# Gate and up projections of a streaming encoder: sixteen of twenty-two column tiles by seven block products on a pre-normed x, and a down projection over all its outputs at once

## The chip, the cores and the metric

The kernel runs on one core of one Trainium2 chip, in one launch. The metric is the time on the device in microseconds (us); the kernel before takes 2091.73 us, the median of three runs (2091.29 to 2091.8). TensorE (PE in the profile) multiplies matrices into PSUM, eight banks of 128 rows by 512 fp32; VectorE (DVE), ScalarE (ACT) and GpSimd (POOL) work element by element; SyncE (SP) issues most of the DMAs. Each engine works through its own queue in order and waits for the others at semaphores.

## What is computed

Two layers on x of 512 frames by 1024 features. Each has a half-step SwiGLU feed-forward block (FFN), a mixer (three attention variants between two projections) and a second FFN; a last RMSNorm follows. The FFN, to which the change belongs:

```python
def rmsnorm(x, g):
    y = x * rsqrt(mean(x * x, axis=-1, keepdims=True) + EPS)
    return y * g

def swiglu(x, w_gate, w_up, w_down):          # 1024 x 2816, 1024 x 2816, 2816 x 1024
    return (silu(x @ w_gate) * (x @ w_up)) @ w_down

x = x + 0.5 * swiglu(rmsnorm(x, ffn1_norm), ffn1_w_gate, ffn1_w_up, ffn1_w_down)
...
x = x + 0.5 * swiglu(rmsnorm(x, ffn2_norm), ffn2_w_gate, ffn2_w_up, ffn2_w_down)
```

Everything is float32. The kernel reaches that precision with three passes of the rounded type fp32r: a value v is split into vh (v rounded) and vl = v - vh, and a product is the sum of wh*xh, wh*xl and wl*xh.

## The kernel before

x stands transposed: eight tiles x[k] of 128 features by 512 frames (KD = 8), beside them the split halves xh[k] and xl[k]. The hidden width of 2816 is 22 column tiles of 128 (KF = 22).

**Weights.** `plan` lists every weight unit in the order of use. `load_unit` (lines 109 to 131) takes the next: one DMA on SP's queue brings 128 x 1024 fp32 (512 KB) into `raw`, ACT copies it to `wh` (line 125), DVE subtracts to get `wl` (line 130). All of these tiles share eight buffers (`WBUFS`), and `wunit` keeps two units ahead of the one in use.

**One product.** `mm3` (lines 144 to 148) is three matmuls, each with a weight load of 128 x 128 (PEld in the profile) and, in the FFN, a moving operand of 128 x 512.

**One FFN** (lines 257 to 329). The gain is applied to x before the split, but 1/rms, which differs from frame to frame, is not: it is kept in `rbc` and multiplied in at the end. Gate and up are made in column groups (`UP_GROUPS`: two tiles, then four at a time). While the first group runs, POOL ends the sum of squares, `norm_stats` sums it over the partitions by matmuls (`ps_st`, line 210), and `norm_rows` broadcasts it (`ps_bc`, line 220). `evict` (lines 270 to 278) takes a tile's gate and up from PSUM: two multiplies by `rbc`, a silu on ACT, a product, and the split of the hidden tile into `fh` and `fl`. The down product follows in two halves of four output tiles (`DOWN_GROUPS`), each over all 22 hidden tiles; `norm_tile` then adds to the sum of squares and splits the new x for the next stage. The last FFN of the net makes its output with frames on the partitions (`last_down`) and puts the eight transposes of x for that (`token_x`) among the first group's matmuls.

**Order.** The program is written stage by stage; the framework's scheduler decides in which order the instructions of neighbouring steps stand on each engine, and pools with a fixed number of buffers decide what waits for what.

Of the kernel before, what the change touches and what calls it, by code (L numbers as in the profile page):

```python
# [9 lines left out]
F32 = mybir.dt.float32  # L10
# [19 lines left out]
UP_GROUPS = [(0, 2)] + [(j, 4) for j in range(2, KF, 4)]  # L30
DOWN_GROUPS = [(0, 4), (4, 4)]
# [18 lines left out]
class Net:  # L50
# [19 lines left out]
    def plan(self):  # L70
# [9 lines left out]
        def ffn(which, l, last=False):  # L80
# [3 lines left out]
            if last:  # L84
                yield from cols("down", a[f"{which}_w_down"][l], KF, 0, D)
                return
            for m, nm in DOWN_GROUPS:
                yield from cols("down", a[f"{which}_w_down"][l], KF, m * P, nm * P)

        for l in range(self.depth):  # L90
# [16 lines left out]
            yield from ffn("ffn2", l, l == self.depth - 1)  # L107

    def load_unit(self):
# [4 lines left out]
        name, src, nk, n = u  # L114
        m = nk * n
# [15 lines left out]
        self.ahead.append((name, v(wh), v(wl)))  # L131

# [18 lines left out]
    def constants(self):  # L151
# [21 lines left out]
        self.gains = keep.tile([P, P], F32, name="gains")  # L173
# [56 lines left out]
    def start(self, xp):  # L230
        nc = self.nc
        self.xt = [xp.tile([P, NT, 256], F32, name=f"xt{q}") for q in range(4)]
# [24 lines left out]
    def ffn(self, next_norm, begin=False):  # L257
        nc = self.nc
        with self.tc.tile_pool(name="ff", bufs=1, reuse_waits="tile") as fp:
            fh = [fp.tile([P, T], F32R, name=f"fh{j}") for j in range(KF)]  # L260
            fl = [fp.tile([P, T], F32R, name=f"fl{j}") for j in range(KF)]
            if not next_norm:
                self.rows = [fp.tile([P, D], F32, name=f"row{t}") for t in range(NT)]

            if begin:
                self.start(fp)
                self.first_x(0, ("ffn1_norm", 0))
                self.first_x(1, ("ffn1_norm", 0))

            def evict(j, gate, up):  # L270
                g = fp.tile([P, T], F32, name="g", tag="g", bufs=2)
                u = fp.tile([P, T], F32, name="u", tag="u", bufs=2)
                nc.vector.tensor_mul(g, gate, self.rbc)
                nc.scalar.activation(g, g, AF.Silu)
                nc.vector.tensor_mul(u, up, self.rbc)
                nc.vector.tensor_mul(u, u, g)  # L276
                nc.scalar.activation(fh[j], u, AF.Copy)  # L277
                nc.vector.tensor_sub(fl[j], u, f32(fh[j]))

            first = True  # L280
            for j, nj in UP_GROUPS:
                ps = {}
# [732 lines left out]
```

## Time and profile before

| | kernel before |
|---|---|
| three runs | 2091.29, 2091.73, 2091.8 us |
| the profiled execution | 2092.02 us; its span is 2090.2 us, so 1.8 us lie around it |
| TensorE busy | 2055.3 us (98%), 9801 matmuls, each with its load |
| VectorE busy | 1109.7 us (53%) |
| ScalarE busy | 830.7 us (40%) |
| GpSimd busy | 231.2 us (11%) |
| chain that ended last | PE 84%, DVE 8%, ACT 3% |

The four FFNs take about seven tenths of the span; the two mixers lie at about 390 to 700 and 1420 to 1735 us. A matmul's duration in the profile (0.40 us at 512 columns) is longer than the distance to the next one's start, since matmuls are pipelined; costs on TensorE are therefore read from starts.

### The profile page before, as it was taken

What the parts mean: (1) busy time and instruction counts of PE and PEld (TensorE: products, weight loads), DVE (VectorE), ACT (ScalarE), POOL (GpSimd) and SP (SyncE); (2) the same over time, 40 slices, a digit from 0 to 9 for tenths busy, and PEclk for the clock granted to TensorE, in tenths of its full rate; (3) what the DMA queues carried; (4) which work ended last, traced back from release to release, by engine and by line L of the source; (5) the groups of instructions that cost most, each with busy time, mean ns of one, the idle gap of its engine ahead of it and who ended that gap; (6) DMA issues with size and microseconds to landing.
All of it is one profiled execution on the core that took longest, in us unless ns stands there. A gap on an engine that the chain in (4) does not pass through costs nothing.

```text
span 2090.2 us, 25620 instructions
## 1 busy us (share of the span) xinstructions
PE 2055.3 (98%) x9801; PEld 1709.2 (82%) x9801; DVE 1109.7 (53%) x2000; ACT 830.7 (40%) x1398; POOL 231.2 (11%) x279
## 2 busy tenths in 40 slices
PE   7999999999999999999999999999999999999998
PEld 6888888898887888888888888889988888888886
DVE  4444433599986444543254454236999863544423
ACT  4222222376675322322232233225666843322222
POOL 2000000113433100000010000001233330000000
PEclk9999999999999999999999999999999999999999
DMA  4333323322212333333333333223222123333322
GB/s 137 91 94 98 91 94 98 89 74 61 68 54 65 91 98 94 91 99 93 91 91 100 91 91 100 92 90 85 79 59 56 51 83 99 95 97 91 100 92 91
DMA packets 112230, 183.09 MB, mean 88 GB/s; under 512 B 6242, under 2 KB 45484, under 8 KB 112108
## 3 DMA queue, kind: packets, MB, share of 16 engines
q1 hardware_dynamic: 111132, 179.59, 29.2%
q8 instruction: 77, 1.26, 0.3%
q10 hardware_dynamic: 864, 1.57, 0.2%
q14 instruction: 45, 0.37, 0.1%
q0 software_dynamic: 112, 0.30, 0.0%
HBM read 179.34 MB, written 2.10 MB: 87 GB/s over the span
## 4 chain that ended last, share of the span: by engine, by line
PE 84%; DVE 8%; ACT 3%; issue 2%; DMA 1%; POOL 1%; DVEq 0%; POOLq 0%; ACTq 0%; SPq 0%
PE ps_f L147 15%; PE ps_f L148 15%; PE ps_f L146 15%; PE ps_d L146 8%; PE ps_d L148 7%; PE ps_d L147 7%; PE ps_p L146 2%; PE ps_p L147 2%; PE ps_p L148 2%; PE ps_s L776 1%; PE ps_w L147 1%; PE ps_w L148 1%; PE ps_w L146 1%; PE ps_pt L449 1%; DVE isc L551 1%
## 5 line engine op out<-in xcount | busy, mean ns | idle before, releaser
L130 DVE TENSOR_TENSOR wl<-raw,wh 128x1024 fp32r<-128x1024 f32 (+5 forms) x323 | 388.1, 1202 | 840.6 <-PE ps_f L147 450.8
L125 ACT ACTIVATE wh<-raw 128x1024 fp32r<-128x1024 f32 (+5 forms) x346 | 355.5, 1028 | 836.0 <-DMA raw<-in_ffn_w_down 321.7
L146 PE MATMUL ps_f<-xh,wh 128*128 128x512 f32 x1408 | 558.6, 397 | 1.3 <-ACT xh L203 1.3
L147 PE MATMUL ps_f<-xl,wh 128*128 128x512 f32 x1408 | 558.1, 396 | 0.6 <-DVE xl L204 0.5
L148 PE MATMUL ps_f<-xh,wl 128*128 128x512 f32 x1408 | 557.3, 396 | 0.0
L147 PEld LDWEIGHTS ps_f<-xl,wh 128*128 128x128 f32 x1408 | 265.1, 188 | 65.3 <-DVE xl L204 2.1
L146 PEld LDWEIGHTS ps_f<-xh,wh 128*128 128x128 f32 x1408 | 264.8, 188 | 64.7 <-ACT xh L203 1.6
L148 PEld LDWEIGHTS ps_f<-xh,wl 128*128 128x128 f32 x1408 | 265.1, 188 | 63.7
L148 PE MATMUL ps_d<-fh,wl 128*128 128x512 f32 x528 | 208.8, 396 | 0.0
L147 PE MATMUL ps_d<-fl,wh 128*128 128x512 f32 x528 | 208.8, 395 | 0.0
L146 PE MATMUL ps_d<-fh,wh 128*128 128x512 f32 x528 | 208.8, 395 | 0.0
L198 POOL TENSOR_TENSOR rbc<-rbc,sq 128x512 f32<-128x512 f32 x42 | 63.6, 1515 | 1095.5 <-ACT sq L197 1094.7
L146 PE MATMUL ps_p<-wh,xh 128*128 128x320 f32 (+3 forms) x448 | 145.3, 324 | 2.1 <-ACT itm L466 1.5
L147 PE MATMUL ps_p<-wl,xh 128*128 128x320 f32 (+3 forms) x448 | 140.6, 314 | 0.0
L148 PE MATMUL ps_p<-wh,xl 128*128 128x320 f32 (+3 forms) x448 | 140.5, 314 | 0.0
L147 PEld LDWEIGHTS ps_d<-fl,wh 128*128 128x128 f32 x528 | 99.3, 188 | 24.0
L148 PEld LDWEIGHTS ps_d<-fh,wl 128*128 128x128 f32 x528 | 99.3, 188 | 24.0
L146 PEld LDWEIGHTS ps_d<-fh,wh 128*128 128x128 f32 x528 | 99.3, 188 | 23.8
L277 ACT ACTIVATE fh<-u 128x512 fp32r<-128x512 f32 x88 | 55.1, 630 | 130.7 <-DVE u L276 130.3
L786 POOL TENSOR_SCALAR s<-s,sm 128x128 f32<-128x128 f32 (+3 forms) x128 | 77.3, 606 | 225.2 <-DVE sm L785 188.1
L784 ACT ACTIVATE s<-s,sm 128x128 f32<-128x128 f32 (+3 forms) x128 | 71.6, 560 | 45.9 <-DVE sm L782 44.7
L146 PEld LDWEIGHTS ps_p<-wh,xh 128*128 128x128 f32 x448 | 84.3, 188 | 4.6 <-ACT itm L466 3.0
(204 smaller groups left out, 2739.1 us busy)
## 6 DMA issues: line engine op xcount, KB each, us to landing
raw<-in_ffn_w_gate SPq DMA_DIRECT2D x88, 512.0 KB, 3.7
raw<-in_ffn_w_up SPq DMA_DIRECT2D x88, 512.0 KB, 3.7
raw<-in_ffn_w_down SPq DMA_DIRECT2D x88, 512.0 KB, 3.7
raw<-in_w_out SPq DMA_DIRECT2D x32, 256.0 KB, 2.9
raw<-in_w_in SPq DMA_DIRECT2D x16, 384.0 KB, 3.3
raw<-in_w_in SPq DMA_DIRECT2D x12, 512.0 KB, 4.0
raw<-in_w_in SPq DMA_DIRECT2D x12, 480.0 KB, 3.6
xt<-in_x SPq DMA_DIRECT2D x4, 512.0 KB, 9.4
```

The source lines that it names most:

```text
L125: nc.scalar.activation(wh[:, :m], raw[:, :m], AF.Copy)
L130: nc.vector.tensor_sub(wl[:, :m], raw[:, :m], f32(wh[:, :m]))
L146: mm(ps, sh, mh, start=first, stop=False)
L147: mm(ps, sh, ml, start=False, stop=False)
L148: mm(ps, sl, mh, start=False, stop=last)
L198: (engine or nc.gpsimd).tensor_add(self.sacc, self.sacc, sq)
L277: nc.scalar.activation(fh[j], u, AF.Copy)
L449: self.nc.tensor.transpose(out, src, self.ident)
L551: nc.vector.match_replace(out=self.isc[t], in_to_replace=m8, in_values=self.isc[t], imm_value=TAKEN)
L776: nc.tensor.matmul(ps[:, :wm], q[:, t * P:(t + 1) * P], k[:, :wm], start=i == 0, stop=i == len(passes) - 1)
L784: nc.scalar.activation(s, s, AF.Exp, bias=nm, scale=-1.0, accum_out=su)
L786: nc.gpsimd.tensor_scalar(s, s, rc, 1.0, op0=ALU.mult, op1=ALU.mult)
```

## The change

The first six hidden tiles of each FFN are made as before, with one difference: as soon as 1/rms is known, `scale_x` makes the finished normed x (`xn`), and from the second group on xh and xl are its halves, so no later eviction multiplies by `rbc`. For this `norm_stats` stands earlier, after the first 24 matmuls of the first group (in the very first FFN after the first half of its up product).

The other sixteen hidden tiles are made in eight pairs. Left matrix of a pair: A, the gate and up weights of two column tiles, cut into 2 x 2 blocks (rows: first or second tile; columns: first or second 512 features). Right matrix: B, the normed x, cut into 2 x 2 blocks (features; first or second 256 frames). A*B takes seven block products in place of eight, by Strassen's scheme in Winograd's form, with four sums S1 to S4 of weight blocks per pair, four sums T1 to T4 of x blocks once per FFN, and seven additions of results. Each block product holds its gate and its up part side by side in one PSUM bank and is 24 matmuls with 256 moving columns. The sums are made in fp32 and split afterwards. Hidden tiles are kept as fp32 (`u`) and split, two at a time, in the down stage, which now makes all eight outputs together and holds the last three hidden tiles back, so that output after output ends. `token_x` stands in the last pair.

```diff
-UP_GROUPS = [(0, 2)] + [(j, 4) for j in range(2, KF, 4)]
-DOWN_GROUPS = [(0, 4), (4, 4)]
+UP_GROUPS = [(0, 2), (2, 4)]
+PAIRS = range(6, KF, 2)
+SEVEN = ("A11", "A12", "S2", "S1", "S3", "S4", "A22")
+H = T // 2
+HELD = 3
...
+            for j in PAIRS:
+                for i, name in enumerate(SEVEN):
+                    yield name, j, 0, 0
+                    if i == 2 and j + 2 < KF:
+                        yield "pair", (which, l, j + 2), 0, 0
+            yield from cols("down", a[f"{which}_w_down"][l], KF, 0, D)
...
+    def load_pair(self, which, l, j):
+        halves = []
+        for h in range(2):
+            raw = self.fp.tile([P, 2, 4, 2, P], F32, name="raw2", tag="rw", bufs=3)
+            for g, w in enumerate(("gate", "up")):
+                src = self.a[f"{which}_w_{w}"][l][h * T:(h + 1) * T, j * P:(j + 2) * P]
+                self.nc.sync.dma_start(raw[:, g].rearrange("p k i c -> p k (i c)"),
+                                       src.rearrange("(k p) c -> p k c", p=P))
+            halves.append(raw.rearrange("p g k i c -> p (g k) i c"))
+        self.raws[j] = {f"A{i + 1}{h + 1}": halves[h][:, :, i] for i in range(2) for h in range(2)}
+
+    def block_sum(self, j, name):
+        r = self.raws[j]
+        if name not in r:
+            a, op, b = {"S1": ("A21", ALU.add, "A22"), "S2": ("S1", ALU.subtract, "A11"),
+                        "S3": ("A11", ALU.subtract, "A21"), "S4": ("A12", ALU.subtract, "S2")}[name]
+            a, b = self.block_sum(j, a), self.block_sum(j, b)
+            r[name] = self.fp.tile([P, 1024], F32, name=name, tag="sums", bufs=2).rearrange("p (k c) -> p k c", c=P)
+            self.nc.vector.tensor_tensor(r[name], a, b, op=op)
+        return r[name]
+
+    def operand(self, name, j):
+        nc, v = self.nc, self.block_sum(j, name)
...
+        nc.scalar.activation(wh, v, AF.Copy)
+        nc.vector.tensor_sub(wl, v, f32(wh))
+        self.ahead.append((name, wh, wl))
...
+                            if first and i == 1 and k0 == 0 and w == ("up" if begin else "gate"):
+                                self.norm_stats()
+                            if first and i == 1 - begin and k0 == 4 and w == ("up" if begin else "gate"):
+                                self.norm_rows()
+                                self.scale_x(norm)
...
+    def scale_x(self, norm):
+        self.xn = [self.fp.tile([P, 4, T], F32, name=f"xn{h}", tag="rw", bufs=3) for h in range(2)]
+        for k in range(KD):
+            self.nc.vector.scalar_tensor_tensor(self.xn[k // 4][:, k % 4], self.x[k], self.gain(*norm, k), self.rbc,
+                                                op0=ALU.mult, op1=ALU.mult)
...
+        for name, x, y in (("T1", "B12", "B11"), ("T2", "B22", "T1"), ("T3", "B22", "B12"), ("T4", "B21", "T2")):
...
+            nc.vector.tensor_sub(b[name], b[x], b[y])
...
+            nc.scalar.activation(th, b[name], AF.Copy)
+            nc.vector.tensor_sub(tl, b[name], f32(th))
...
+    def seven(self, left, right):
+        mm = self.nc.tensor.matmul
+        wh, wl = self.wunit(left)
+        self.turn = not self.turn
+        ps = self.ps("at" if self.turn else "pj", "ps_s7")
+        for g in range(2):
+            out = ps[:, g * H:(g + 1) * H]
+            for k in range(4):
+                sh, sl = wh[:, 4 * g + k], wl[:, 4 * g + k]
+                mh, ml = self.right[right](k)
+                mm(out, sh, mh, start=k == 0, stop=False)
+                mm(out, sh, ml, start=False, stop=False)
+                mm(out, sl, mh, start=False, stop=k == 3)
+        return ps
...
+        def block(i, c, v):
+            g = self.small.tile([P, T], F32, name="sg", tag="sq", bufs=2)[:, :H]
+            nc.scalar.activation(g, v[:, :H], AF.Silu)
+            nc.vector.tensor_mul(u[:, i, c * H:(c + 1) * H], v[:, H:], g)
+
+        v = tmp("v")
+        nc.scalar.activation(v, self.seven("A11", "B11"), AF.Copy)
+        c11 = tmp("c11")
+        add(c11, self.seven("A12", "B21"), v)
+        block(0, 0, c11)
+        add(v, self.seven("S2", "T2"), v)
+        p5, c12 = self.seven("S1", "T1"), tmp("c12")
+        add(c12, p5, v)
+        add(v, self.seven("S3", "T3"), v)
+        c22 = tmp("c22")
+        add(c22, p5, v)
+        block(1, 1, c22)
+        add(c12, self.seven("S4", "B22"), c12)
+        block(0, 1, c12)
+        if rows:
+            self.token_x()
+        add(v, self.seven("A22", "T4"), v)
+        block(1, 0, v)
...
+        self.nc.scalar.activation(z[:, 0], u[j], AF.Copy)
+        self.nc.vector.tensor_sub(z[:, 1], u[j], f32(z[:, 0]))
```

Three places show how the instructions stand now. VectorE between two groups of gate and up in the first FFN, before (`ps_f` are the gate and up tiles in PSUM, `g` and `u` their evicted forms, `fl` the low half of a hidden tile):

```order
L273 TENSOR_TENSOR g_683<-ps_f_427,rbc_164 128x512
L278 TENSOR_TENSOR fl2_97<-u_656,fh2_75 128x512
L276 TENSOR_TENSOR u_670<-u_670,g_669 128x512
L275 TENSOR_TENSOR u_684<-ps_f_551,rbc_164 128x512
L273 TENSOR_TENSOR g_697<-ps_f_428,rbc_164 128x512
```

VectorE in the fifth pair of the first FFN, in the changed kernel (`ps_s7` is a block product, `ol` the low half of a left operand, `S` a sum of weight blocks; the third S, S1_1904, belongs to the next pair):

```order
L164 TENSOR_TENSOR S3_1737<-raw2_1457 128x1024
L173 TENSOR_TENSOR ol_1740<-S3_1737,oh_1739 128x1024
L421 TENSOR_TENSOR c11_1697<-ps_s7_1708,v_1662 128x512
L164 TENSOR_TENSOR S4_1769<-raw2_1460,S2_1665 128x1024
L416 TENSOR_TENSOR u7_80<-c11_1697,sg_1734 128x256
L423 TENSOR_TENSOR v_1662<-ps_s7_1743,v_1662 128x512
L173 TENSOR_TENSOR ol_1772<-S4_1769,oh_1771 128x1024
L173 TENSOR_TENSOR ol_1803<-raw2_1460,oh_1802 128x1024
L425 TENSOR_TENSOR c12_1800<-ps_s7_1775,v_1662 128x512
L164 TENSOR_TENSOR S1_1904<-raw2_1698,raw2_1701 128x1024
L173 TENSOR_TENSOR ol_1838<-raw2_1698,oh_1837 128x1024
```

Where VectorE took tiles out of PSUM and split hidden tiles, it now makes sums of weights, splits operands and adds results in one interleaved row; the split of S3 stands right behind S3's sum, and S1 of the next pair needs both halves of that pair's weights.

SyncE's queue in the same stage of the changed kernel (`raw2_1457` and `raw2_1460` are the two halves of one pair's weights, the next two those of the pair after):

```order
L152 DMA raw2_1460<-in_ffn1_w_gate 128x4x256 [waits DMAHW5_49,DMAHW6_49,DVE_49,Activation_49]
L152 DMA raw2_1460<-in_ffn1_w_up 128x4x256
L152 DMA raw2_1698<-in_ffn1_w_gate 128x4x256 [waits DMAHW7_49,DMAHW0_49,DVE_49]
L152 DMA raw2_1698<-in_ffn1_w_up 128x4x256
L152 DMA raw2_1701<-in_ffn1_w_gate 128x4x256 [waits DMAHW1_49,DMAHW2_49,DVE_49,Activation_49]
```

Three buffers turn among the halves: the second half of a pair takes the buffer of the previous pair's first half, so its two loads wait until VectorE and ScalarE have done with that half, whose last reader is the sum S3.

TensorE at the start of the second FFN, before:

```order
L148 MATMUL ps_f_6133<-xh7_154,wl_6105 128x512
L210 MATMUL ps_st_6183<-ones_126,rbc_164 128x1 x4
L146 MATMUL ps_f_6134<-xh4_151,wh_6104 128x512
L147 MATMUL ps_f_6134<-xl4_159,wh_6104 128x512
L148 MATMUL ps_f_6134<-xh4_151,wl_6105 128x512
```

and in the changed kernel, after the first 24 matmuls of that FFN:

```order
L191 MATMUL ps_f_6871<-xh3_117,wl_6773 128x512
L253 MATMUL ps_st_6902<-ones_93,rbc_131 128x1 x4
L189 MATMUL ps_f_6870<-xh4_118,wh_6802 128x512
L190 MATMUL ps_f_6870<-xl4_126,wh_6802 128x512
L191 MATMUL ps_f_6870<-xh4_118,wl_6803 128x512
```

The `ps_st` matmuls, which read the sum of squares, stood behind 84 matmuls of the FFN and now stand behind 24.

## Rows read from the trace of the kernel before

**Rows 1.** The profile's page: the span, the busy times, TensorE's granted clock in 40 slices (9 is 90% or more of full speed), and the shares of the chain that ended last.

```profile
span 2090.2 us, 25620 instructions
...
PE 2055.3 (98%) x9801; PEld 1709.2 (82%) x9801; DVE 1109.7 (53%) x2000; ACT 830.7 (40%) x1398; POOL 231.2 (11%) x279
...
PEclk9999999999999999999999999999999999999999
...
PE 84%; DVE 8%; ACT 3%; issue 2%; DMA 1%; POOL 1%; DVEq 0%; POOLq 0%; ACTq 0%; SPq 0%
```

**Rows 2.** The windows view: the third FFN from its second group to near its end, and the first mixer. Columns: the stretch, its length, busy us of each engine with instructions, granted clock, DMA share, GB/s.

```profile
755.00:1059.00 304.00, 304.00 (x1304) 244.62 (x1303) 123.38 (x135) 85.22 (x102) 11.30 (x7) 1.00 0.33 95
410.00:700.00 290.00, 282.71 (x1639) 251.08 (x1638) 241.96 (x622) 193.72 (x423) 90.06 (x114) 1.00 0.24 69
```

**Rows 3.** The view by lines, shapes kept apart: one of the three matmul lines of gate and up, and its weight loads. Columns: line, engine, operation, tiles, shapes, count, busy us, mean ns of one, idle time before.

```profile
L146 PE MATMUL ps_f<-xh,wh 128*128 128x512 f32 x1408 | 558.6, 397 | 1.3 <-ACT xh L203 1.3
...
L146 PEld LDWEIGHTS ps_f<-xh,wh 128*128 128x128 f32 x1408 | 264.8, 188 | 64.7 <-ACT xh L203 1.6
```

**Rows 4.** The timeline of TensorE where narrower matmuls follow each other in the mixers: ten starts of 288 columns (the first and the last), a run of 256 columns in each mixer (the first of the run and what follows it, here the 384 wide one that ends it), and two of the weight loads in the first run. Columns: start us, duration us, instruction.

```profile
436.46 0.29 PE L146 MATMUL ps_p<-wh,xh 128*128 128x288 f32 x1
...
437.66 0.30 PE L146 MATMUL ps_p<-wh,xh 128*128 128x288 f32 x1
...
466.31 0.28 PE L776 MATMUL ps_s<-ckh,cql 96*128 96x256 f32 x1
...
466.67 0.34 PE L776 MATMUL ps_s<-ckl,cqh 96*128 96x384 f32 x1
...
1497.48 0.28 PE L776 MATMUL ps_s<-ckh,cql 96*128 96x256 f32 x1
...
1497.83 0.34 PE L776 MATMUL ps_s<-ckl,cqh 96*128 96x384 f32 x1
...
466.32 0.19 PEld L776 LDWEIGHTS ps_s<-ckl,cqh 96*128 96x128 f32 x1
466.44 0.19 PEld L776 LDWEIGHTS ps_s<-ckh,cql 96*128 96x128 f32 x1
```

**Rows 5.** The view by lines, VectorE: a subtraction of 1024 elements per partition, two products of 512 (one from PSUM, one of SBUF tiles), a subtraction of 256, and a product with a column and a tile.

```profile
L130 DVE TENSOR_TENSOR wl<-raw,wh 128x1024 fp32r<-128x1024 f32 x278 | 345.2, 1242 | 810.0 <-PE ps_f L147 450.8 <-PE ps_d L147 270.9 <-ACT wh L125 40.2
L275 DVE TENSOR_TENSOR u<-ps_f,rbc 128x512 f32<-128x512 f32 x88 | 60.3, 686 | 7.0 <-PE ps_f L148 7.0
...
L278 DVE TENSOR_TENSOR fl<-u,fh 128x512 fp32r<-128x512 f32 x88 | 59.8, 684 | 14.5 <-ACT fh L277 14.4
...
L801 DVE TENSOR_TENSOR pt<-ps_pt,pt 128x256 fp32r<-128x256 f32 x32 | 13.3, 414 | 0.2
...
L411 DVE SCALAR_TENSOR_TENSOR row<-row,m,x 128x512 f32<-128x512 f32 x8 | 5.7, 747 | 2.7 <-POOL m L408 2.7
```

**Rows 6.** The same view, ScalarE: a copy of 1024 elements, one of 512 and one of 256 from PSUM.

```profile
L125 ACT ACTIVATE wh<-raw 128x1024 fp32r<-128x1024 f32 x292 | 309.2, 1059 | 804.4 <-DMA raw<-in_ffn_w_down 321.7 <-DMA raw<-in_ffn_w_up 251.9 <-DMA raw<-in_ffn_w_gate 212.4
...
L374 ACT ACTIVATE row<-ps_y 128x512 f32<-128x512 f32 x8 | 4.7, 590 | 4.9 <-PE ps_y L373 4.8
...
L800 ACT ACTIVATE pt<-ps_pt 128x256 fp32r<-128x256 f32 x32 | 12.0, 374 | 2.8 <-PE ps_pt L449 2.6
```

**Rows 7.** The timeline of VectorE at two places where an instruction follows another without a wait.

```profile
678.70 1.23 DVE L130 TENSOR_TENSOR wl<-raw,wh 128x1024 fp32r<-128x1024 f32 x1
679.84 1.79 DVE L204 SCALAR_TENSOR_TENSOR xl<-x,gains,xh 128x512 fp32r<-128x512 f32 x1
...
704.10 0.68 DVE L275 TENSOR_TENSOR u<-ps_f,rbc 128x512 f32<-128x512 f32 x1
704.70 0.68 DVE L273 TENSOR_TENSOR g<-ps_f,rbc 128x512 f32<-128x512 f32 x1
```

**Rows 8.** The timeline at the start of the second and the fourth FFN: TensorE's first matmul of the FFN and, of the second, its 25th; GpSimd's last addition to the sum of squares.

```profile
678.56 0.39 PE L146 MATMUL ps_f<-xh,wh 128*128 128x512 f32 x1
...
684.15 0.40 PE L146 MATMUL ps_f<-xh,wh 128*128 128x512 f32 x1
...
684.80 1.31 POOL L198 TENSOR_TENSOR rbc<-rbc,sq 128x512 f32<-128x512 f32 x1 [2.02 <-ACT sq L197]
...
1709.77 0.39 PE L146 MATMUL ps_f<-xh,wh 128*128 128x512 f32 x1
...
1715.90 1.29 POOL L198 TENSOR_TENSOR rbc<-rbc,sq 128x512 f32<-128x512 f32 x1 [2.02 <-ACT sq L197]
```

**Rows 9.** The timeline in the first FFN (GpSimd's last addition, `ps_st`, the copy of `rbc`) and one of the eight transposes of x in the last.

```profile
31.52 1.29 POOL L198 TENSOR_TENSOR rbc<-rbc,sq 128x512 f32<-128x512 f32 x1 [1.03 <-ACT sq L197]
...
38.34 0.83 PE L210 MATMUL ps_st<-ones,rbc 128*128 128x1 f32 x7
...
42.72 0.60 ACT L221 ACTIVATE rbc<-ps_bc 128x512 f32<-128x512 f32 x1 [2.16 <-PE ps_bc L220]
...
1712.57 0.60 PE L373 MATMUL ps_y<-ident,x 128*128 128x128 f32 x4
```

**Rows 10.** The DMA view of 660 to 690 us, where the loads come in pieces of 1 KB as those of the pairs do: GB/s in 40 slices of 0.75 us, and the issues with count, size and median us from issue to landing.

```profile
GB/s 0 0 22 0 61 208 375 55 0 0 0 30 76 363 229 0 0 0 0 57 302 332 8 0 0 0 53 184 384 78 0 0 0 27 98 399 175 0 0 0
...
raw<-in_ffn_w_gate SPq DMA_DIRECT2D x3, 512.0 KB, 3.9
```

More of the change, by code (lines that the diff above doesn't have):

```diff
@@ L78, in cols, with ffn @@
                 yield name, w[k0 * P:(k0 + nk) * P, c0:c0 + n], nk, n
-        def ffn(which, l, last=False):
+        def ffn(which, l):
             for j, nj in UP_GROUPS:
@@ L83, in ffn @@
                     yield from cols(w, a[f"{which}_w_{w}"][l], KD, j * P, nj * P)
[L84 to L88, printed above, removed]
+                    if j and w == "gate":
+                        yield "pair", (which, l, PAIRS[0]), 0, 0
+            for j in PAIRS:
[4 more added lines that the diff above has]
+            yield from cols("down", a[f"{which}_w_down"][l], KF, 0, D)
         for l in range(self.depth):
@@ L114, in load_unit @@
         name, src, nk, n = u
+        if name == "pair":
+            self.load_pair(*src)
+            return self.load_unit()
+        if name in SEVEN:
+            return self.operand(name, src)
         m = nk * n
@@ L231, in start @@
         nc = self.nc
-        self.xt = [xp.tile([P, NT, 256], F32, name=f"xt{q}") for q in range(4)]
+        self.xt = [xp.tile([P, NT, 256], F32, name="xt", tag="t", bufs=8) for q in range(4)]
         self.constants()
@@ L309, in ffn @@
                     for i in range(nj):
[L310 to L329 removed]
+                        evict(j + i, ps["gate"][i], ps["up"][i], True)
@@ new lines, in ffn @@
+                    self.sums_x()
+            self.turn = True
+            for j in PAIRS:
+                self.pair(u[j // 2], not next_norm and j + 2 == KF)
+            (self.down if next_norm else self.last_down)(u, next_norm)
+    def scale_x(self, norm):
+        self.xn = [self.fp.tile([P, 4, T], F32, name=f"xn{h}", tag="rw", bufs=3) for h in range(2)]
+        for k in range(KD):
+            self.nc.vector.scalar_tensor_tensor(self.xn[k // 4][:, k % 4], self.x[k], self.gain(*norm, k), self.rbc,
+                                                op0=ALU.mult, op1=ALU.mult)
@@ new lines, in pair @@
+    def pair(self, u, rows):
+        nc = self.nc
+        add = nc.vector.tensor_add
+        tmp = lambda name: self.fp.tile([P, T], F32, name=name, tag="g", bufs=4)
+        def block(i, c, v):
[20 more added lines that the diff above has]
+        block(1, 0, v)
@@ L399, in last_down @@
                 c = slice(h * T, (h + 1) * T)
-                for i in range(held):
-                    piece(KF - held + i, t, h, ws[i])
+                for k in range(KF - HELD, KF):
+                    piece(k, t, h)
                 nc.vector.scalar_tensor_tensor(row[:, c], ps[t][h], 0.5, row[:, c], op0=ALU.mult, op1=ALU.add)
```

155 lines of the change are left out of this document (89 added, 66 removed).

## The prediction

> **What bounds the kernel now.** I read the page first. TensorE is busy 2055.3 of 2090.2 us, its clock is granted at nine tenths or more in every slice (full speed, 2.4 GHz), and the chain that ended last is PE for 84% [rows 1]. Then the windows, stage by stage: within an FFN, 755 to 1059 us, TensorE is busy without a gap, VectorE 41% and ScalarE 28%; only in a mixer does VectorE reach 83% [rows 2]. So in the FFNs, where the change is, TensorE alone sets the time, and the question is what a matmul costs. The same row gives it: 304.00 us over 1304 matmuls, 0.2331 us from start to start at 512 columns. The durations of 397 ns [rows 3] overlap and are not to be summed.
>
> **The change, part by part.**
>
> *Products.* A pair of hidden tiles took 2 tiles x 2 matrices x 8 x 3 = 96 matmuls of 512 columns; it now takes 7 x 24 = 168 of 256. Over 8 pairs and 4 FFNs: 3072 go and 5376 come. The 3072 cost 3072 x 0.2331 = 716 us. For 256 columns the mixers have short runs: three in 466.67 - 466.31 = 0.36 us and three in 0.35 us, so 0.117 to 0.120 us each [rows 4]. At 288 columns nine follow in 1.20 us, 0.133 each [rows 4]; the slope from there to 512 is (0.2331 - 0.1333)/224 = 0.446 ns a column, which puts 256 at 0.119. I take 0.119: 640 us. That saves 76 us. The bounds: 0.117 saves 87 us, and 0.1333, the step of the narrowest shape seen in a longer row, saves nothing.
>
> What speaks against 0.119 is the weight load: 188 ns each [rows 3], longer than the matmul's share of time. But in the run of 256 columns loads start 0.12 us apart at that same duration [rows 4], so they overlap one another as well as the matmuls, and I let them cost nothing more. The Trainium skill (TensorE: Matmul & The Clock Gate, Part 3: Packing small matmuls) says that a load overlaps matmuls in flight only where it goes to another row group; these loads fill all rows, so by that rule every load would stand bare before its matmul. The trace disagrees already at 512 columns, where the step is 0.233 us and a stream of that width with a bare load of 188 ns could not be. The measurement decides; what the rule would make of this change is the third rival.
>
> *VectorE in a pair.* Four sums and seven splits of 1024 elements (1242 ns), seven additions of 512 (686), four products of 256 (414) [rows 5]: 13.7 + 4.8 + 1.7 = 20.1 us. Two instructions that wait for nothing overlap: 679.84 - 678.70 = 1.14 us instead of 1.23, and 0.60 instead of 0.68 [rows 7], some 0.08 each, so 22 of them come to 18.3 us. One wait cannot be hidden: the split of S3 stands directly behind S3's sum and between them ScalarE must copy it, 1.06 us [rows 6] and two handovers, together some 1.2. That is 19.5 us beside TensorE's 168 x 0.119 = 20.0. So TensorE still sets the pace, by a hair; I take 20.0 for a pair. The upper end: nothing overlaps, and each of the four 256-products waits for its silu (0.37 us [rows 6] and a handover, 0.5): 20.1 + 1.2 + 2.0 = 23.3 us. In each pair VectorE stands in line for TensorE's products, and behind each such addition the next operands' splits are queued; the operands are prepared three products ahead, 3 x 2.86 us, so a late addition of a microsecond or two reaches TensorE only if it recurs in every pair.
>
> *ScalarE.* Seven copies, one eviction and four silus: 7 x 1.06 + 0.59 + 4 x 0.37 = 9.5 us [rows 6], half of the pair. Costs nothing.
>
> *Loads.* A pair needs the same 2 MB as before, as four loads. The second half's two wait for S3 of the pair before, and S1 of the next pair needs them. One load with 1 KB pieces lands after 3.9 us, and a slice at 375 to 399 GB/s moves 0.29 MB in 0.75 us, so the second is in some 1.4 us later [rows 10]: 5.3 us, at worst 7.8 in series. From S1 to the next S3 lie, in the first two or three pairs of an FFN (S1 stands before the next product's addition there), 8 x 1.16 + 6 x 0.60 + 3 x 0.33 = 13.9 us of VectorE; with S3 itself the ring is 1.2 + 5.3 + 13.9 = 20.4, in later pairs (S1 stands some 3.5 us later) 17. Against 20.0 that costs at most 0.4 us a pair, which the lead of three products swallows: 0. With 7.8 us it would be 22.9, and 12 pairs would lose up to 35 us; that end is kept.
>
> *Sum of squares sooner.* In the second FFN the matmuls of `ps_st` now stand at the 25th place, 684.15 us by the old clock, while GpSimd ends its last addition at 684.80 + 1.31 = 686.11; in the fourth 1709.77 + 5.59 = 1715.36 against 1717.19 [rows 8]. TensorE waits there, and everything behind `ps_st` in its queue with it: 2.0 + 1.8, say 4 us. In the first FFN GpSimd is done at 32.81, and `ps_st` moves 12 matmuls up from 38.34 to 35.5 [rows 9]: no wait.
>
> *Normed x.* After `rbc`, VectorE makes eight products of 0.75 us, eight splits of 0.68 and six evictions of 0.69 [rows 5] while TensorE still has 24 matmuls (in the first FFN 12) of the first group and then the second group's first 24 with two of the eight x tiles. Where 24 are left it fits. In the first FFN `rbc` now ends at 43.32 - 2.8 = 40.5 [rows 9], the splits at 40.5 + 8 x 0.67 + 8 x 0.60 = 50.7, the first gate tile leaves PSUM at 51.3; TensorE ends the group at 45.3 and needs that bank 12 matmuls later, at 48.1: 3 us. The sums T1 to T4 and their splits (8 x 1.16 = 9.3 us) and the ten products of the evictions lie under the 45 us of the second group; the loads of its up tiles are queued on SP behind the first pair's second half, which waits for T3. By the same counting they land 1 us before or after they are due: 1 us an FFN, 4 in all, with 0 to 3 each as bounds.
>
> *Down.* The same 2112 matmuls of 512 columns, so nothing; and where the third FFN follows, its `ps_st` needs an addition of 0.69, a square of some 0.6 and GpSimd's 1.31 us after the last of them [rows 5, 6, 8], while 24 matmuls, 5.6 us, pass first: no wait. The eight groups of transposes of x, 0.60 us each [rows 9], stood apart and now come in one row through four banks, each of which ScalarE must empty in 0.59 us [rows 6]; the last four wait for copies, some 0.5 us each: 2 us.
>
> *Sum.* The profiled execution took 2092.0 us (span 2090.2 and 1.8 around it), 0.3 above the median of the runs: 2092.0 - 76 + 4 + 3 + 4 + 2 = 2029 us.
>
> **The rivals.**
>
> First, VectorE sets the pace, but by less than the gain: the waits are real and the overlap is gone. At 20.1 + 1.2 = 21.3 us a pair, 1.3 us x 32 pairs more: 2029 + 42 = 2071; from 20.5 to 22.0 it would be 2045 to 2093. For it speaks that VectorE's 19.5 us leave no reserve, against it that the overlap is seen wherever nothing waits.
>
> Second, slower: the same queue at 23.3 us a pair, 3.3 x 32 = 106 more: 2135 us. The old pair took 96 x 0.2331 = 22.4; with the 13 us of small losses the kernel is slower from 22.0 on. It needs every silu to be waited for in full, though the order puts other work between addition and product in most places.
>
> Third, the weight loads bind: no two overlap, and a matmul takes 188 ns [rows 3]. Then 5376 x 0.188 = 1011 us come for 716: 2092 + 295 + 13 = 2400 us. Slower from 0.131 us a matmul on. Against it stand the runs at 0.12 [rows 4], which are only three long.
>
> Fourth, the gain and the losses cancel, for instance pairs at 22.0: 2092 us.
>
> **How the numbers follow.** My forecast (TensorE paces the pairs, 2012 to 2045) 0.70; VectorE paces with some gain 0.16, half of it under 2070; the same, slower than before, 0.08; loads bind 0.04; cancelled 0.02. Predicted is the first, 2029. The range of 8 in 10 goes from 2010, where 256 columns cost 0.117 us and the small losses vanish partly, to 2070: 0.70 and half of 0.16 are 0.78, and the rest is what lies close above. Its lower end would need a step under 0.116 us to be missed. 0.2% is 4 us, about what a measurement of this kernel can tell from no change: faster 0.86, same 0.02, slower 0.12.
>
> **What the profile after would show.** Right: 5376 `ps_s7` matmuls starting 0.119 us apart with hardly any idle; VectorE above 90% in the pairs, waiting for PE more than PE for it; a TensorE wait of about 2 us before `ps_st` in the second and fourth FFN and 3 us before a `ps_f` in the first; each FFN some 16 us shorter, the mixers as they were. Wrong: regular idle on PE before `ps_s7` ended by `ol` or `oh` (VectorE paces), S1 waiting for `raw2` (the loads' ring), or `ps_s7` starts above 0.13 us without a wait (weight loads).

## The result, and the profile after

The changed kernel takes 2027.3 us, the median of four runs (2023.93, 2025.89, 2028.71, 2030.12); the kernel before took 2091.77 beside it (2091.29 to 2092.01). The ratio is 0.9691, with a 95% interval of 0.9675 to 0.9708: 64 us faster. The prediction was 2029. The profiled execution is the fastest of the four, with a span of 2022.2 us against 2090.2.

The page of the profile after, in the order of [rows 1]: span, busy times, granted clock by slices, the three matmul groups of the pairs and one group of their weight loads (busy time, mean ns, idle before); left-out lines are marked:

```profile
span 2022.2 us, 30973 instructions
PE 1973.1 (98%) x12105; PEld 1759.4 (87%) x12105; DVE 1470.4 (73%) x2404; ACT 979.1 (48%) x1594; POOL 229.3 (11%) x279
...
PEclk9999999999999999999999999999999999999999
...
L403 PE MATMUL ps_s<-xh,ol 128*128 128x256 f32 x768 | 215.9, 281 | 0.0
L401 PE MATMUL ps_s<-xh,oh 128*128 128x256 f32 x768 | 215.6, 281 | 0.0
L402 PE MATMUL ps_s<-xl,oh 128*128 128x256 f32 x768 | 215.5, 281 | 0.0
...
L402 PEld LDWEIGHTS ps_s<-xl,oh 128*128 128x128 f32 x768 | 144.7, 188 | 0.2
```

VectorE has gone from 53% to 73% of the span, and still TensorE is at 98%. How close it is inside the pairs, the windows of the first, second and last FFN's eight pairs show (columns: PE, PEld, DVE, ACT, POOL busy, granted clock, DMA share, GB/s):

```profile
90.80:246.60 155.80, 155.80 (x1345) 155.75 (x1344) 142.94 (x171) 74.23 (x95) 0.00 (x0) 1.00 0.30 99
734.80:890.40 155.60, 155.60 (x1345) 155.60 (x1344) 143.03 (x171) 74.07 (x95) 0.00 (x0) 1.00 0.30 98
1729.00:1890.70 161.70, 159.78 (x1377) 159.07 (x1377) 145.09 (x175) 79.65 (x105) 0.00 (x0) 1.00 0.30 97
```

In the second row TensorE is busy for all of 155.60 us with 1344 matmuls: 0.1158 us each, 19.45 us a pair. VectorE is busy 143.03 of it, 92%. What VectorE waits for in that stretch is, above all, ScalarE's copy before a split, 1.2 us a pair (waits view; us in all, times, longest):

```profile
DVE ol L173 <- ACT oh L172: 9.8, 13, 1.2
```

No wait of VectorE for a block product stands in that view. The last FFN has the transposes of x in its last pair and 6 us more.

Where the 68.0 us of span come from, read as distances between the first matmuls of the stages in the two traces (in the kernel before the mixers end at 678.6 and 1709.8 us; the later ends given above take in the start of an FFN):

| stage | before | after | difference |
|---|---|---|---|
| start to the first up matmul | 12.85 | 9.84 | -3.0 |
| gate and up, FFN 1, 2, 3, 4 | 253.6, 248.05, 247.9, 251.2 | 236.8, 227.8, 226.1, 233.7 | -16.8, -20.2, -21.8, -17.5 |
| down, FFN 1 to 3 | 123.2 each | 123.2 each | 0 |
| down, FFN 4, to its last matmul's start | 120.62 | 122.97 | +2.35 |
| from there to the end | 8.68 | 8.44 | -0.24 |
| mixers | 288.9, 288.9 | 292.75, 294.1 | +3.85, +5.2 |

Four places lose time that could be told in the rows. At the start of the second FFN TensorE waits for GpSimd's last addition, and some 2 us later it falls to half speed (timeline; the idle time before an instruction and its releaser stand in brackets):

```profile
667.97 0.40 PE L191 MATMUL ps_f<-xh,wl 128*128 128x512 f32 x1
670.23 1.05 PE L253 MATMUL ps_st<-ones,rbc 128*128 128x1 f32 x8 [1.86 <-POOL rbc L241]
671.14 0.48 PE L189 MATMUL ps_f<-xh,wh 128*128 128x512 f32 x1
...
672.41 0.63 PE L191 MATMUL ps_f<-xh,wl 128*128 128x512 f32 x1
672.84 0.63 PE L189 MATMUL ps_f<-xh,wh 128*128 128x512 f32 x1
673.26 0.63 PE L190 MATMUL ps_f<-xl,wh 128*128 128x512 f32 x1
...
675.40 0.57 PE L189 MATMUL ps_f<-xh,wh 128*128 128x512 f32 x1
675.81 0.40 PE L190 MATMUL ps_f<-xl,wh 128*128 128x512 f32 x1
```

The wait, 2.03 us by the starts (the bracket counts from the end of the matmul before), was predicted. The eight matmuls from 672.41 on, 0.427 us apart in place of 0.233, were not: the granted clock is at 1.2 GHz there, and they cost 1.5 us more. The fourth FFN shows the same (1.86 us of wait, 1.5 us of slow matmuls), the third a wait of 0.92 us and no fall. In the first FFN TensorE waits for the first new split of x, behind eight scalings on VectorE, and pays 1.7 us at the low clock as well:

```profile
43.93 0.50 PE L190 MATMUL ps_f<-xl,wh 128*128 128x512 f32 x1 [3.50 <-DVE xl L373]
```

```profile
37.88 5.39 DVE L367 SCALAR_TENSOR_TENSOR xn<-x,gains,rbc 128x512 f32<-128x512 f32 x8 [1.79 <-ACT rbc L264]
43.18 4.91 DVE L373 TENSOR_TENSOR xl<-xn,xh 128x512 fp32r<-128x512 f32 x8
48.00 0.69 DVE L315 TENSOR_TENSOR g<-ps_f,rbc 128x512 f32<-128x512 f32 x1
```

And the first product of each mixer waits for its weights' lower half, which the forecast had not foreseen:

```profile
369.87 0.30 PE L189 MATMUL ps_p<-wh,xh 128*128 128x296 f32 x1
371.98 0.40 PE L190 MATMUL ps_p<-wl,xh 128*128 128x296 f32 x1 [1.82 <-DVE wl L141]
```

The windows of the 6 us behind that wait, in the first and in the second mixer: the same work and the same wait of 2 us, but only in the second did the clock fall (0.72), so that fewer matmuls fit in (31 in place of 40):

```profile
371.90:378.00 6.10, 5.77 (x40) 5.54 (x41) 5.58 (x9) 3.81 (x6) 2.92 (x2) 1.00 0.18 54
1365.00:1371.00 6.00, 5.86 (x31) 5.86 (x32) 5.47 (x8) 3.80 (x6) 2.91 (x2) 0.72 0.17 54
```

In the last pair of the last FFN the transposes of x wait twice, 0.8 and 1.6 us by their starts, for PSUM banks whose block products VectorE has not yet added (`c`); the last five groups follow without a wait:

```profile
1881.93 1.03 PE L515 MATMUL ps_y<-ident,x 128*128 128x128 f32 x8
1883.54 0.63 PE L515 MATMUL ps_y<-ident,x 128*128 128x128 f32 x4 [0.57 <-DVE c L428]
1885.51 2.57 PE L515 MATMUL ps_y<-ident,x 128*128 128x128 f32 x20 [1.35 <-DVE c L430]
```

### The profile page after: what moved, and what is told of

It reads as the page before. It is cut to its first block, busy times and chain, and to the rows that moved or that the text cites. A ratio compares the mean times of both kernels' runs of the same rounds, so it can differ in the third digit from the quotient of the medians.

```text
span 2022.2 us, 30973 instructions
## 1 busy us (share of the span) xinstructions
PE 1973.1 (98%) x12105; PEld 1759.4 (87%) x12105; DVE 1470.4 (73%) x2404; ACT 979.1 (48%) x1594; POOL 229.3 (11%) x279
## 4 chain that ended last, share of the span: by engine, by line
PE 80%; DVE 9%; ACT 4%; issue 3%; DMA 1%; POOL 1%; DVEq 0%; POOLq 0%; SPq 0%; ACTq 0%
PE ps_s L401 10%; PE ps_s L402 10%; PE ps_s L403 10%; PE ps_d L190 7%; PE ps_d L191 7%; PE ps_d L189 7%; PE ps_f L191 4%; PE ps_f L190 4%; PE ps_f L189 4%; PE ps_p L189 2%; PE ps_p L190 2%; PE ps_p L191 2%; PE ps_s L922 2%; DMA raw<-in_w_in 1%; PE ps_w L190 1%
## 5 line engine op out<-in xcount | busy, mean ns | idle before, releaser
L141 DVE TENSOR_TENSOR wl<-raw,wh 128x1024 fp32r<-128x1024 f32 (+6 forms) x195 | 234.1, 1201 | 353.7 <-PE ps_d L190 241.7
L136 ACT ACTIVATE wh<-raw 128x1024 fp32r<-128x1024 f32 (+6 forms) x218 | 219.7, 1008 | 333.3 <-DMA raw<-in_ffn_w_down 243.7
L403 PE MATMUL ps_s<-xh,ol 128*128 128x256 f32 x768 | 215.9, 281 | 0.0
L401 PE MATMUL ps_s<-xh,oh 128*128 128x256 f32 x768 | 215.6, 281 | 0.0
L402 PE MATMUL ps_s<-xl,oh 128*128 128x256 f32 x768 | 215.5, 281 | 0.0
L191 PE MATMUL ps_d<-fhl,wl 128*128 128x512 f32 x528 | 208.9, 396 | 0.0
L190 PE MATMUL ps_d<-fhl,wh 128*128 128x512 f32 x528 | 208.8, 396 | 0.0
L189 PE MATMUL ps_d<-fhl,wh 128*128 128x512 f32 x528 | 208.8, 395 | 0.0
L190 PE MATMUL ps_f<-xl,wh 128*128 128x512 f32 x384 | 154.5, 402 | 4.0 <-DVE xl L373 3.5
L189 PE MATMUL ps_f<-xh,wh 128*128 128x512 f32 x384 | 154.4, 405 | 1.4 <-ACT xh L246 0.9
L191 PE MATMUL ps_f<-xh,wl 128*128 128x512 f32 x384 | 152.2, 402 | 0.1
```

The costliest lines, as they stand in the source:

```text
L136: nc.scalar.activation(wh[:, :m], raw[:, :m], AF.Copy)
L141: nc.vector.tensor_sub(wl[:, :m], raw[:, :m], f32(wh[:, :m]))
L189: mm(ps, sh, mh, start=first, stop=False)
L190: mm(ps, sh, ml, start=False, stop=False)
L191: mm(ps, sl, mh, start=False, stop=last)
L401: mm(out, sh, mh, start=k == 0, stop=False)
```

## The experiments

Every kernel below was timed beside the kernel before (2089.5 to 2090.02 us there). Stage times are from the profiles.

### Which part brings the gain: no block products

```diff
-UP_GROUPS = [(0, 2), (2, 4)]
-PAIRS = range(6, KF, 2)
+UP_GROUPS = [(0, 2)] + [(j, 4) for j in range(2, KF, 4)]
+PAIRS = range(0)
...
-                    self.sums_x()
-            self.turn = True
-            for j in PAIRS:
-                self.pair(u[j // 2], not next_norm and j + 2 == KF)
+            if not next_norm:
+                self.token_x()
```

> The changed kernel, with all 22 column tiles made by plain products of 512 columns again (one group of two, five of four); the pre-normed x and the down product over all outputs at once stay. Theory (the pairs' saving is the matmuls' alone, at the measured steps): the 3072 matmuls of 512 columns cost 3072 x 0.2331 = 716 us where the pairs take 628.6 us in the profile after, so the span rises from 2022 by some 88 to 91 us, to 2110 to 2113. By the price of the prediction (256 columns at 0.119 us) it would rise by 76, to 2098. Rival: a good part of the gain comes from the rest of the change or from the start; then it is well under 2098, towards 2090.

Measured: 2113.59 us (2111.01 to 2115.14), ratio 1.0109 (1.0094 to 1.0124); span 2113.4, 91.2 above the changed kernel. The theory's number came. So the seven products alone bring 86 to 91 us, more than the 76 of the prediction, and what came with them, the normed x, the earlier sums and the down product over all outputs, makes the kernel slower by itself: 23.6 us over the kernel before. Its mixers take 4.0 and 6.4 us longer than in the kernel before, as in the changed kernel, so their loss has nothing to do with the pairs. And its 32 transposes of x, in one row through the same four banks and with the same copies by ScalarE, ran without a wait:

```profile
1980.03 3.66 PE L511 MATMUL ps_y<-ident,x 128*128 128x128 f32 x32
```

### Who sets the pace of a pair: VectorE's work taken away

```diff
-            a, b = self.block_sum(j, a), self.block_sum(j, b)
+            r[name] = self.block_sum(j, {"S1": "A21", "S2": "A11", "S3": "A22", "S4": "A12"}[name])
+            return r[name]
```

> The changed kernel without the four sums S1 to S4 of weight blocks in each pair: a raw block stands in for each, so the hidden tiles of the pairs are not the reference's; the number of splits, products and result additions is the same. VectorE loses 4 x 1.14 = 4.6 us of the 17.9 it is busy in a pair. Theory (TensorE sets the pace of the pairs): each pair still takes 168 x 0.1159 = 19.5 us, and the span stays at 2022 within 3 us. Rival (VectorE sets the pace, and TensorE only looks full): the pairs fall with VectorE's work, by up to 4.6 x 32 = 146 us in all, but not under the products' own time if the step were shorter than 0.1159.

Measured: 2020.29 us (2018.53 to 2022.68); span 2017.8. The window of the second FFN's pairs:

```profile
735.95:891.50 155.55, 155.55 (x1345) 155.55 (x1344) 117.54 (x144) 75.58 (x97) 0.00 (x0) 1.00 0.31 98
```

VectorE's busy time in this window falls by 25.5 us and the pairs take the same 155.55. TensorE sets the pace. Of the 4.4 us that the whole span is shorter, two lie in the last pair: there the transposes of x find their banks emptied in time, and it takes 23.3 in place of 25.5 us:

```profile
1879.84 3.90 PE L516 MATMUL ps_y<-ident,x 128*128 128x128 f32 x32
```

### How much is left on VectorE: a little added, and more

```diff
         nc.vector.tensor_sub(wl, v, f32(wh))
+        if name in ("A11",):
+            nc.vector.tensor_sub(wl, v, f32(wh))
```

> The changed kernel with one instruction more on VectorE in each pair: the split of A11 is written twice (1.14 us). In the profile after VectorE is busy 17.9 of the 19.5 us of a pair, and waits 1.1 to 1.2 us for ScalarE's copy of S3. Theory (that wait cannot be filled, reserve 0.4 us): VectorE becomes the pace, 19.5 + 1.14 - 0.4 = 20.2 us a pair, 0.7 x 32 = 23 us more, span 2045. Rival (the wait shrinks when VectorE runs behind, reserve 1.6 us): the extra instruction is hidden and the span stays at 2022 to 2026.

The same with `("A11", "S4")`:

> The changed kernel with two instructions more on VectorE in each pair: the splits of A11 and of S4 are written twice (2.28 us). Theory (reserve 0.4 us): 1.9 us more in each of 32 pairs, 60 us, span 2082. Rival (reserve 1.6 us): 0.7 x 32 = 22 us, span 2044. In both the step from one extra instruction to two is at most 1.14 x 32 = 36 us.

And with the last product of 256 elements written twice:

> The changed kernel with one small instruction more on VectorE in each pair: the last product of 256 elements is written twice (0.33 us); ScalarE's order stays as it is. Theory (TensorE sets the pace and VectorE has some reserve in its waits): the pairs stay at 155.5 to 156 us in the first three FFNs. Rival (VectorE is already the pace): 0.33 us in each of 32 pairs, 11 us or more, pairs at 158.3 or above.

Measured: 2074.99 us with one more (2073.33 to 2077.36), 2111.55 with two (2109.92 to 2112.73), 2025.63 with the small one (2023.16 to 2028.15). The windows of the second FFN's pairs, with the small one and with one large one:

```profile
738.50:894.10 155.60, 155.60 (x1345) 155.56 (x1344) 145.12 (x178) 74.18 (x95) 0.00 (x0) 1.00 0.29 96
```

```profile
748.70:918.60 169.90, 162.78 (x1345) 159.42 (x1344) 153.23 (x180) 74.20 (x96) 0.00 (x0) 0.99 0.28 88
```

0.33 us a pair are hidden in full in the second and third FFN (155.6 us for the eight pairs). In the first the pairs took 157.0 us, 1 us more than expected; with unchanged pairs other kernels took 155.8 to 156.7 there, so whether the addition shows in it is open. 1.14 us are not hidden at all. They cost 48 us by the medians and 49 by the profiles, 1.5 us a pair, more than the instruction is long and twice what the theory had; the second costs another 36.6 us, 1.14 x 32, as long as it is. So VectorE's reserve is at least 0.33 us a pair, and both numbers of the expectation for one instruction were wrong. Why more than its length: VectorE is busy 19.2 us of a pair of 21.2, so its waits have grown from 1.6 to 2.1 us. With the extra instruction the scheduler also put ScalarE's silus of a pair in a row, ahead of copies that VectorE needs, and the waits are those of the two engines for each other (waits view of the window with one large instruction; us in all, times, longest):

```profile
ACT oh L172 <- DVE S L164: 38.9, 20, 3.3
ACT sg L417 <- DVE c L430: 19.2, 8, 4.8
DVE ol L173 <- ACT oh L172: 10.9, 18, 2.3
...
PEld ps_s L405 <- DVE ol L173: 6.1, 7, 1.9
```

How much of the 1.5 us is the new order and how much the instruction wasn't told apart, so it isn't shown that 1.14 us would be too much with ScalarE's order kept. The small addition left that order as it was.

### The early sums: later in the second to fourth FFN

```diff
-if first and i == 1 and k0 == 0 and w == ("up" if begin else "gate"):
+if first and (i == 1 and k0 == 0 and w == "up" if begin else i == 1 and k0 == 4 and w == "gate"):
     self.norm_stats()
-if first and i == 1 - begin and k0 == 4 and w == ("up" if begin else "gate"):
+if first and i == 0 and k0 == (4 if begin else 0) and w == "up":
     self.norm_rows()
```

> The changed kernel, in the second to fourth FFN with the sums over the partitions (ps_st) after 48 instead of 24 matmuls of the first group and the broadcast (ps_bc) and the normed x after 60 instead of 48. Theory (TensorE waits there for GpSimd's last addition, and the fall of the granted clock to half that follows comes from this wait): the waits of 2.03, 0.92 and 1.86 us go, and in the second and fourth FFN the eight to nine matmuls at 0.427 us too, 1.5 us each: 7.8 us less, span 2014. Rival 1: the fall of the clock hangs on the eight matmuls of one column, not on the wait: it stays, 4.8 us less, span 2017. Rival 2: the wait moves on to the second group, whose split of x now comes later: 0 to 4 us less, with a new TensorE wait for xl.

Measured: 2022.57 us (2020.1 to 2026.18); span 2018.3, 3.9 less than the changed kernel's and not 7.8. The 288 matmuls of 512 columns that open an FFN take 68.8, 71.6 and 68.7 us in the second, third and fourth, in place of 71.9, 70.0 and 71.8. The window of the opening of the second FFN after, and here:

```profile
662.40:734.80 72.40, 70.54 (x303) 56.63 (x302) 48.82 (x54) 29.36 (x39) 5.74 (x4) 0.98 0.35 109
```

```profile
665.60:735.00 69.40, 69.32 (x303) 55.52 (x302) 48.51 (x54) 29.79 (x39) 5.78 (x4) 1.00 0.36 114
```

and the eight matmuls of one column, now without a wait before them:

```profile
677.37 0.95 PE L253 MATMUL ps_st<-ones,rbc 128*128 128x1 f32 x8
```

In the second and fourth FFN wait and slow matmuls go together, 3.1 us each, though the same eight small matmuls are still there: rival 1 falls, the clock fell because of the wait. In the third FFN rival 2 holds: three new waits for weight halves take the place of the one, and it is 1.6 us slower:

```profile
1019.86 0.50 PE L189 MATMUL ps_f<-xh,wh 128*128 128x512 f32 x1 [0.29 <-ACT wh L136]
1021.42 0.50 PE L191 MATMUL ps_f<-xh,wl 128*128 128x512 f32 x1 [0.83 <-DVE wl L141]
...
1062.68 0.50 PE L189 MATMUL ps_f<-xh,wh 128*128 128x512 f32 x1 [0.75 <-ACT wh L136]
```

### The first FFN: splits between the scalings

```diff
 self.norm_rows()
-self.scale_x(norm)
+if begin:
+    self.scale_x(norm, range(2))                 # scales and splits
+    for q in range(2):
+        nc.vector.tensor_mul(gates[q], ps["gate"][q], self.rbc)
+    self.scale_x(norm, range(2, 4))
...
+                    if begin:
+                        self.scale_x(norm, range(4, KD))
```

> The changed kernel, in the first FFN with another order on VectorE after rbc: two x tiles scaled and split, the two gate tiles multiplied out of PSUM, and then the other six x tiles, in place of eight scalings, eight splits and then the evictions. Theory (TensorE waits 3.67 us for the first split because eight scalings stand ahead of it, and pays 1.7 us more at the lower clock): the wait shrinks to under 0.5 us and the clock stays: 5 us less, the first 288 matmuls in 75 to 76 us in place of 80.7. Rival (another wait takes its place, for a PSUM bank or for a later split): 0 to 2 us less.

Measured: 2023.21 us (2017.87 to 2027.98). The opening takes 77.87 us in place of 80.71:

```profile
12.72:90.80 78.08, 75.35 (x323) 59.13 (x324) 54.26 (x62) 38.84 (x54) 10.82 (x8) 1.00 0.34 109
```

The wait of 3.7 us and the slow matmuls behind it are gone and the granted clock is 1.00 in place of 0.98, but 2.8 us are won and not 5: three smaller waits, 1.2, 0.9 and 0.6 us, stand later in the second group. Between theory and rival. The size is rough: in the eight profiles with this opening unchanged it took 79.7 to 81.7 us, in the three with the new order 77.0 to 77.9.

### The mixers: two hidden tiles held in place of three

```diff
-HELD = 3
+HELD = 2
```

> The changed kernel with two hidden tiles held back at the end of each down product in place of three. Theory (the first wl of the mixer is late because its buffer is held: three held units keep six of the eight weight buffers, and raw and wh of the next unit fill the other two): with four held, wl is made before the eight x tiles come, the wait of 2.0 us at the start of each mixer goes, 4 us less, mixers at 290.5 and 292. Rival (VectorE is late because the adding and splitting of eight x tiles in a row, stretched beside GpSimd, fills it): the x tiles now follow one another after 6 matmuls, 1.4 us, in place of 9, 2.1 us, the wait stays at 2 us or grows.

Measured: 2020.09 us (2018.56 to 2021.15); span 2019.4. In VectorE's row the first `wl` of the mixer is made at 361.21, ahead of the x tiles; in the changed kernel it stood at 370.86, behind the sixth of them (first the row of the kernel with two held, then of the changed kernel):

```profile
361.21 1.08 DVE L141 TENSOR_TENSOR wl<-raw,wh 128x888 fp32r<-128x888 f32 x1 [4.37 <-PE ps_d L190]
362.79 0.69 DVE L468 SCALAR_TENSOR_TENSOR x<-ps_d,x 128x512 f32<-128x512 f32 x1 [0.49 <-PE ps_d L191]
```

```profile
369.17 1.77 DVE L247 SCALAR_TENSOR_TENSOR xl<-x,gains,xh 128x512 fp32r<-128x512 f32 x1
370.86 1.07 DVE L141 TENSOR_TENSOR wl<-raw,wh 128x888 fp32r<-128x888 f32 x1
```

The wait at the mixer's start is gone, and the mixers take 289.2 and 287.7 us in place of 292.5 and 293.9 (from first to last start): 9.4 us less, as much as they had lost: the two waits of 2 us, the low clock behind one of them, and the rest in later waits that I did not follow one by one. So holding three tiles back was the cause. That it acts through the buffers is the count of the theory (six of eight kept), which this result fits; a kernel with more buffers was not run. The rival's fear came true elsewhere: where the third FFN follows, the x tiles come too fast for GpSimd, and its sums wait 3.2 us in place of 0.9, with seven slow matmuls behind:

```profile
1021.62 1.05 PE L253 MATMUL ps_st<-ones,rbc 128*128 128x1 f32 x8 [2.99 <-POOL rbc L241]
...
1023.41 0.63 PE L189 MATMUL ps_f<-xh,wh 128*128 128x512 f32 x1
1023.84 0.63 PE L190 MATMUL ps_f<-xl,wh 128*128 128x512 f32 x1
```

### The same kernel again, and the parts together

> The changed kernel once more, word for word, for what differs from run to run. Its own four runs went from 2023.93 to 2030.12 us, and the start (first matmul of the first group at 9.8 to 12.9 us in the profiles so far) and the last down product (0.2289 or 0.2333 us a matmul) differ between kernels that issue the same there. Theory (these two are chance of the run, not the change's doing): a second profile of the same kernel shows other values in one or both, and the stages in between within 0.3 us of the first profile. Rival (they hang on the kernel's own order or buffers): start 9.84 and 0.2333 us again.

> The changed kernel with what the single runs bore out: the interleaved order in the first FFN (2.8 us), later sums over the partitions in the second and fourth FFN alone (3.1 us each; in the third it cost 1.6), and two hidden tiles held back before a mixer (3.3 and 6.1 us) but three before the third FFN (where two cost 3.1). Theory (the losses lie in different stages and add up): 18 us less than the changed kernel in the same call. Rival (what is won in one stage is waited for in the next): 10 us less or fewer.

```diff
-            self.token_x()
+            self.token_x(range(4, 8))           # and range(4) behind S3's product
```

> The combined kernel, and in the last pair the eight groups of transposes of x stand as four and four, 24 matmuls apart, in place of eight in a row. Theory (in a row, the last four wait for banks that ScalarE empties): the last FFN's pairs take 159 to 160 us in place of 161.6 to 164.5, 2 to 4 us less than the combined kernel. Rival (other waits of ScalarE or VectorE in that pair set its time): the pairs stay above 161.5 us.

Measured: the changed kernel again 2025.32 us (2024.66 to 2026.79), ratio 0.969 (0.9677 to 0.9704); combined 2008.07 (2006.71 to 2009.48), ratio 0.9607 (0.9594 to 0.962); with the transposes spread 2007.47 (2006.59 to 2007.68), ratio 0.9603 (0.959 to 0.9616).

The second profile of the same kernel has its first up matmul at 10.25 us, the last down product at 0.2289 us a matmul (0.2333 in the first profile) and the last FFN's pairs at 165.1 us (161.6, from first to last start). The other openings, pairs and down products agree within 0.8 us, the mixers within 1.8 (in this profile the clock stayed up behind both of their first waits), which is more than the 0.3 expected. So the last down product's +2.35 us in the table is chance of the run. The start lay at 9.8 to 12.9 us over all these profiles, in kernels that issue the same there, and I count its -3.0 as chance too. What sets either is open.

The combination wins 17.3 us over the changed kernel beside it, against 18 expected: the losses did lie in separate stages. The opening of the second FFN there:

```profile
659.10:727.80 68.70, 68.64 (x301) 55.16 (x300) 48.22 (x54) 29.66 (x38) 6.20 (x4) 1.00 0.37 115
```

Spreading the transposes won nothing: the pairs of the last FFN took 165.2 us. The two waits at the banks went, but one of 3.4 us came, for a bank whose sum on VectorE (`c`) was late, and half-speed matmuls behind it:

```profile
PE ps_y L535 <- DVE c L446: 3.4, 1, 3.4
ACT sg L431 <- DVE c L448: 3.1, 1, 3.1
DVE c L448 <- PE ps_s L419: 3.0, 1, 3.0
```

The rival holds: that pair is set by the other engines' order, not by the row of transposes alone. The banks waited for were those that VectorE's sums still held, before the spreading too; in the kernels without block products and without the sums S1 to S4 the same row ran without a wait.

## Why the prediction was right, point by point

The time was met (2029 against 2027.3), and the leading mechanism is shown: TensorE sets the pace of the pairs, at all but no idle. Part of the nearness is two errors that cancel, which is luck: with the products at their measured size and the other terms as forecast the sum would have been 2092 - 93 + 13 = 2012 us, near the foot of the range, and losses that were too small or left out brought it back up. By the terms, for the first profile:

| term | predicted | measured |
|---|---|---|
| products | -76 | -93 (5376 x 0.1159 = 623 for 716) |
| sums sooner | +4 | +7.8 (waits 4.8, slow matmuls 3.0) |
| first FFN | +3 | +5.4 (3.7 and 1.7) |
| late loads of the second group | +4 | +0.9 (two waits of 0.46 for a weight copy) |
| transposes of x | +2 | +2.6 (last pair 25.53 - 19.45, less 32 x 0.109) |
| mixers | 0 | +9.1 |
| last down, start | 0 | +2.35, -3.0 (counted as chance) |
| end | 0 | -0.2 |
| sum | -63 | -68 of 68.0 |

*Products.* The term was mis-sized by 17 us: "I take 0.119". The slope from 288 to 512 columns was taken from a run of nine in a mixer; the short runs of 256 columns that I had beside it gave 0.117 to 0.120, and the long row has 0.1158, below both.

*Weight loads.* The third rival is dead: loads of 188 ns follow 0.1158 us apart over 1344 matmuls without idle, so they overlap each other and the matmuls. The rule of the Trainium skill (TensorE: Matmul & The Clock Gate, Part 3: Packing small matmuls), by which a load overlaps only where it goes to another row group, does not hold for these rows; the same part of that page also lets a load into the background weight buffer go ahead of running matmuls, and with that the rows agree.

*VectorE.* "By a hair" was right, and so was the wait for the copy of S3, 1.2 us a pair. The sign "waiting for PE more than PE for it" was not: in the second FFN's pairs the view shows neither waiting for the other, and VectorE waits for ScalarE. The rivals that VectorE sets the pace did not come, but their place is near: with one instruction of 1.14 us more in each pair, and ScalarE's order changed with it, the kernel takes 2075 us, with two 2112, past the kernel before. The prediction's condition, slower from 22.0 us a pair on, fits: at two more the pairs take 22.4.

*Sums sooner.* The waits were as forecast in the second and fourth FFN, 2.03 and 1.86 us for 2.0 and 1.8. Missing were the price of the clock behind them, 1.5 us each, and the wait of 0.92 us in the third FFN, which the prediction had ruled out.

*First FFN.* A wait at a `ps_f` was right, and its size near (3.7 for 3 us), but its cause was another. The prediction let the second group start and wait 12 matmuls later for a PSUM bank; TensorE waited at the group's start, for the first new split of x, which stands behind eight scalings. The nearness of the size is luck, and again the slow matmuls were missing.

*Transposes.* Here too the number was near (2.6 for 2 us) and the reason wrong. The prediction let the last four groups wait for ScalarE's copies; the waits, 0.8 and 1.6 us, were for two banks that VectorE's additions still held, and where those were free the row of 32 transposes ran without a wait.

*Mixers.* The step that failed: "Down: the same 2112 matmuls of 512 columns, so nothing." The prediction counted the instructions of the down product and not what its held tiles keep from the next stage, so it did not see that the lower half of the mixer's first weight unit comes late. The experiment with two held tiles showed it; that buffers are what is kept is argued from their count.

*Loads* of the pairs cost nothing in the changed kernel, as said.

## What to carry to other kernels

When an operand is held back to the end of a stage, count the buffers that it keeps from the next stage's first load, not only the instructions. A wait of 2 us on TensorE in an FFN's opening cost 1.5 us more here, in half-speed matmuls behind it. Where a second engine comes within a tenth of the pace-setter, try it with a small and a large instruction more, and look whether the order on other engines stays: the small one was free here, and the large one, which changed ScalarE's order, cost more than its own length. And when a predicted wait has the right size, read in the trace what ended it: twice here it was not what the forecast named.

## What was not expected of the hardware

- Over the profiles of all changed kernels, TensorE waits of 1.9 to 3.7 us in an FFN's opening were followed in 27 of 28 cases by 5 to 13 matmuls of 512 columns at 1.2 GHz (the exception is the fourth FFN of the kernel without the sums S1 to S4, after 1.86 us); waits of 0.9 to 1.2 us there were not. Behind the wait of about 2 us at a mixer's start, with three tiles held, the clock fell in 5 of 18 cases. Wait length alone does not decide: in the kernel with two large instructions more, waits of 1.1 to 1.5 us within a pair were followed by half speed in three cases. Where the wait in an opening was removed, the fall went with it.
- A matmul of 256 columns, each with a new weight load, steps at 0.1158 us, slightly less than half of the 0.2333 at 512.
- The last down product of the same kernel stepped at 0.2333 us in one profile and 0.2289 in another, in each for the whole product. No cause was found.
